# The Pool's residual maps wait, through a small VectorE read, for the last tile of the normed h

## The chip, the cores and the metric

One NeuronCore of a Trainium2 chip runs the whole program: TensorE (PE), VectorE (DVE), ScalarE (ACT), GpSimd (Pool) and the DMA queues, most of them issued by SyncE (SP). The metric is the device time of one execution in microseconds.

## The reference, cut to what matters

Two transformer blocks run one behind the other on 512 tokens and 256 context tokens, 1024 wide. The change touches only the first block, of two layers. Each layer has a token mixer, an MLP and two LayerNorms that sit on the residual sum:

```
for l in range(2):
    sh1, sc1, g1, sh2, sc2, g2 = split(silu(c) @ w_mod[l] + b_mod[l])
    h = x * (1 + sc1) + sh1                      # and the context alike
    y, yc = token_mixers(h, hc, ...)
    x = layer_norm(ALPHA * x + g1 * y, ln1_g[l], ln1_b[l])
    h = x * (1 + sc2) + sh2
    x = layer_norm(ALPHA * x + g2 * (relu(h @ w_fc1[l])**2 @ w_fc2[l]), ln2_g[l], ln2_b[l])
```

So each LayerNorm gives two things: the modulated h, which the next matmuls read at once, and the new x, which is needed only when the next residual sum is formed.

## The kernel before

Activations lie transposed: eight tiles of 128 channels, and tokens along the free axis. The residual stream R is eight such tiles (768 tokens in layer 0, 512 in layer 1), packed into four or three big tiles (`self.stream`). The tokens are normalised in groups of 256: three groups behind the attention of layer 0, two behind that of layer 1. Matmul operands are pairs hi and lo (`whi`/`wlo` for weights, `hn` for the normed h), and every product takes three matmuls. A weight piece goes through a `wraw` load on SP's queue, a cast to `whi` on ScalarE (L90) and a subtraction to `wlo` on VectorE (L91).

For each group, `LayerNorm` adds the tiles up on Pool (L161, into `ns`), TensorE forms the mean (`lm`, L167 and L168), VectorE and, for two tiles of the eight, Pool subtract it (L174), ScalarE squares (`lq`, L176), and TensorE sums (`lv`, L180). Then `normed` makes h out of each tile: VectorE L1071, ScalarE L1072 (hi), VectorE L1073 (lo). `residual` does not run at once; it puts a function into `self.later`, of two Pool operations that turn R in place into ALPHA times the new x:

```
nc.gpsimd.tensor_tensor(out=z, in0=z, in1=r, op=ALU.mult)             # L1080
nc.gpsimd.tensor_scalar(out=z, in0=z, scalar1=self.dcol(slot, m), ...)  # L1081
```

Below, such a pair of Pool operations is called a pair. `catch_up` runs what is in `self.later`. It is called in `fc1_piece` and at the end of a layer, and finds work there in three places of the program:

- **Place A**, in front of the MLP of layer 0: 24 pairs (three groups of eight).
- **Place B**, between layer 0 and the projections of layer 1: 16 pairs, each with a store of its R tile to the scratch tensor `xa` (128x256, SP's queue, L1422) behind it.
- **Place C**, in front of the MLP of layer 1: 16 pairs.

The engines' instructions are put in order by the scheduler of the tile framework when the kernel is built, out of program order, priorities (weights come first) and dependencies; on the chip each engine and each queue then goes through its list in order.

Names that matter behind the three places. In the MLP, `fc1_piece` makes an activation tile pair `act` out of h: ScalarE L934 (`r`) and L935 (`act`), VectorE L936 and L937. A modulation vector of a later step is computed beside the MLP, as a job of VectorE products: Pool copies one column (L564, from `act` into the buffer `wm`) before SP may load a piece of modulation weights into `wm` (L586), VectorE multiplies and sums it (L574), and L600 finishes the vector. `R<-f,modsb,R` (L973) adds fc2's result to R with the modulation `modsb`. `scale_alpha` (L1350, VectorE) writes the per-channel constants `der` that L1081 reads: slots 8 and 9 are written anew for layer 1 after place A's pairs of layer 0 have read them. Behind place B come the projections `pj`, whose rms norm sums (`pv`, L698) wait for squares of projected tiles.

Of the kernel before, what the change touches and what calls it, by code (L numbers as in the profile page):

```python
# [11 lines left out]
F32 = mybir.dt.float32  # L12
# [3 lines left out]
ALU = mybir.AluOpType  # L16
# [381 lines left out]
class Kernel:  # L398
# [540 lines left out]
    def fc1_piece(self, W, h, groups, pk, sides=(), n=1):  # L939

        ws = [W.get(ahead=n == 1 or i == 0) for i in range(n)]
        acts = [pk.pair() for _ in range(n)]
        pss = [self.P2("f1") for _ in range(n)]
        for i, (c0, c1) in enumerate(groups):
            for side in sides[i:i + 1]:
                self.drain(side)
                if i == len(sides) - 1:
                    self.catch_up()
            for k in range(8):
                for (wh, wl), ps in zip(ws, pss):  # L950
                    s = slice(k * 128, k * 128 + 128)
                    rs = [(c0, c1)] if c1 <= 512 or c0 >= 512 else [(c0, 512), (512, c1)]
                    self.mm3(ps, wh[:, s], wl[:, s], *h[k], rs, k == 0, k == 7)
                    for side in sides[i + 1:]:
                        self.adv(side)
        c0, c1 = groups[0][0], groups[-1][1]
        for act, ps in zip(acts, pss):
            self.relu2(act, ps, c0, c1)
            self.gate = act[0][:, c0:c0 + 1].bitcast(F32)
        return acts  # L960
# [122 lines left out]
                after()  # L1083
        self.later.append(f)

    def catch_up(self):
        while self.later:
            self.later.pop(0)()

# [276 lines left out]
    def block1(self):  # L1366
        nc, a = self.nc, self.a
        W = self.W = Stream(self, *a["stream"], 1)
        between = self.start1()
        h = next(between)  # L1370
        bg = self.bg

        def J(w, tiles, vecs, tag, bias):
            self.tags.add(tag)
            return self.mod_job(w, tiles, vecs, tag, bias)

        both0 = [(0, 0), (1, 1)]
        self.tags |= {"l0.g1", "l0.m2"}
        bg.append(self.mod_groups(range(4, 10), {5: "l0.g1", 9: "l0.m2"}))

        def vectors0():
            self.bcast(1, 1)
            yield

        bg.append(vectors0())
        bg.append(J(a["wmod0"], range(40, 48), both0, "l0.g2", "bmod0"))
        bg.append(J(a["wmod1"], range(0, 16), [(2, 0), (3, 1)], "l1.m1", "bmod1"))
        bg.append(J(a["wmod1"], range(16, 24), [(2, 0)], "l1.g1", "bmod1"))
        bg.append(J(a["wmod1"], range(24, 40), [(2, 0)], "l1.m2", "bmod1"))
        bg.append(J(a["wmod1"], range(40, 48), [(2, 0)], "l1.g2", "bmod1"))  # L1390

        def vectors():
            for slot, v in ((0, 2), (1, 3)):
                self.bcast(v, slot)
                yield

        bg.append(vectors())
        bg.append(J(a["wada0"], range(0, 16), [(4, 0), (5, 1)], "b0.m1", "bada0"))
        for l in range(2):
            last = l == 1  # L1400
            hn, z, gs, groups, sides, norm = self.layer1(l, h, W, between if l == 0 else None)
            h = None
            h2, hpk = [None] * 8, Packer(self, T, name="h")
            state = {}

            def finish(rng, ln, l=l, last=last, h2=h2, hpk=hpk, z=z):
                if last:
                    return self.to_block2(rng, ln, z, h2, hpk)
                if rng[0] == 0:
                    self.need("l1.m1")  # L1410
                    self.fold(4, 2, 0, 1, f"ln2g{l}", f"ln2b{l}")
                    self.fold(6, 3, 0, 1, f"ln2g{l}", f"ln2b{l}")
                    self.scale_alpha(10, f"ln2g{l}")
                    self.scale_alpha(11, f"ln2b{l}")
                s = 6 if rng[0] >= 512 else 4

                def f(m, t, r):
                    if h2[m] is None:
                        h2[m] = hpk.pair()
                    self.normed(h2, m, rng, t, r, s)  # L1420
                    if s == 4:
                        self.residual(m, t, r, 10, lambda: nc.sync.dma_start(out=a["xa"][:, m, rng[0]:rng[1]], in_=t))  # L1422
                return ln.finish(f)

            if last:
                hpk = Packer(self, 512, name="a")
                self.queue2()
            self.run(self.mlp(W, hn, z, gs, groups, sides, norm, finish, f"l{l}.g2"), *RATES[l])
            if last:
                self.need("ctxk")  # L1430
            for i, _ in enumerate(self.side):
                if last and i >= VSKIP and (i - VSKIP) % VEACH == 0:
                    for _ in range(VSTEP):
                        next(self.values, None)
            if last:
                for _ in self.values:
                    pass
            self.catch_up()
            h = h2
        return h  # L1440

# [845 lines left out]
```

## Time and profile before

| | us |
|---|---|
| three runs | 3006.62, 3000.3, 2999.19 |
| median | 3000.3 |
| the profiled execution | 3004.72 |
| its span in the profile | 3002.9 |
| busy in the span: PE, DVE, ACT, POOL | 2825.6 (94%), 1976.0 (66%), 1240.6 (41%), 668.1 (22%) |

The span is what the profiler saw from the first to the last instruction; the rest of the execution's 3004.72 us lies around it. Times in the rows further down are microseconds from the start of the span. Place A lies at 491 to 542, place B at 1075 to 1114 and place C at 1455 to 1491.

### The profile page before, as it was taken

How to read it: one execution, taken by the hardware profiler on the slowest of the kernel's cores; microseconds unless marked ns; L12 is line 12 of the kernel's file. 1: busy time of each engine (PE TensorE's matmuls, PEld its weight loads, DVE VectorE, ACT ScalarE, POOL GpSimd, SP SyncE). 2: the span in 40 equal slices, each digit the busy share in tenths (PEclk: the TensorE clock that was granted, in tenths of full speed). 3: DMA queues.
4: the chain of work that ended last, by engine and by line, in shares of the span. 5: the costliest groups of instructions: out<-in, count | busy, mean ns of one | idle time of the engine just before them, and what ended most of it. 6: DMA issues, size and time to landing. Idle time of an engine off the chain costs nothing.

```text
span 3002.9 us, 40272 instructions
## 1 busy us (share of the span) xinstructions
PE 2825.6 (94%) x15140; PEld 2377.2 (79%) x15140; DVE 1976.0 (66%) x3177; ACT 1240.6 (41%) x2250; POOL 668.1 (22%) x800
## 2 busy tenths in 40 slices
PE   8988999999999989889999999988899999999998
PEld 5877778888888867778887788766788888888887
DVE  3677766676555676886686566677976754664445
ACT  3477663312222244776332333433653223443223
POOL 1134346201000151343511122343310100200001
PEclk9999999999999999999999999999999999899999
DMA  6022221344443321012255555233115542222322
GB/s 251 32 67 70 75 92 41 111 151 165 140 134 126 113 71 39 17 36 79 72 176 173 181 195 179 99 123 109 65 64 195 198 138 99 75 71 98 98 98 71
DMA packets 103072, 329.52 MB, mean 110 GB/s; under 512 B 11708, under 2 KB 18812, under 8 KB 102877
## 3 DMA queue, kind: packets, MB, share of 16 engines
q1 hardware_dynamic: 102300, 325.24, 32.3%
q8 instruction: 120, 1.97, 0.3%
q10 hardware_dynamic: 576, 1.71, 0.2%
q14 instruction: 76, 0.61, 0.1%
HBM read 307.76 MB, written 13.37 MB: 107 GB/s over the span
## 4 chain that ended last, share of the span: by engine, by line
PE 74%; DVE 10%; ACT 5%; issue 5%; DMA 3%; POOL 3%; SPq 0%; DVEq 0%; POOLq 0%; ACTq 0%
PE f L645 47%; PE pj L645 6%; PE op L645 6%; PE s L257 3%; PE acc L346 2%; PE pt L303 1%; DVE st L270 1%; ACT p L280 1%; DVE ptl L335 1%; DVE h L1071 1%; DVE wlo L91 1%; ACT pth L330 1%; PE ms L1095 1%; PE pp L1983 1%; PE lv L180 1%
## 5 line engine op out<-in xcount | busy, mean ns | idle before, releaser
L90 ACT CAST whi<-wraw 128x1024 fp32r<-128x1024 f32 x342 | 358.1, 1047 | 1206.6 <-PE f L645 1004.0
L645 PE MATMUL f<-hn,whi 128*128 128x512 f32 (+1 forms) x2688 | 715.3, 364 | 7.0 <-ACT hn L1072 5.8
L91 DVE TENSOR_TENSOR wlo<-wraw,whi 128x1024 fp32r<-128x1024 f32 x342 | 426.4, 1247 | 341.7 <-ACT whi L90 335.0
L645 PE MATMUL f<-act,whi 128*128 128x512 f32 x2240 | 609.3, 369 | 8.1 <-DVE R L973 8.1
L645 PEld LDWEIGHTS f<-hn,whi 128*128 128x128 f32 x2688 | 467.5, 191 | 90.5 <-ACT hn L1072 7.0
L645 PEld LDWEIGHTS f<-act,whi 128*128 128x128 f32 x2240 | 388.7, 188 | 82.9 <-DVE R L973 9.3
L645 PE MATMUL f<-hn,wlo 128*128 128x512 f32 (+1 forms) x1344 | 446.6, 362 | 0.0
L645 PE MATMUL f<-act,wlo 128*128 128x512 f32 x1120 | 375.8, 368 | 0.0
L973 DVE SCALAR_TENSOR_TENSOR R<-f,modsb,R 128x512 f32<-128x512 f32 (+1 forms) x280 | 188.7, 692 | 132.5 <-PE f L645 132.5
L645 PEld LDWEIGHTS f<-hn,wlo 128*128 128x128 f32 x1344 | 238.7, 191 | 39.1
L564 POOL COPY wm<-act 128x1 f32<-128x1 f32 x152 | 83.4, 555 | 824.2 <-ACT act L935 415.6
L574 DVE SCALAR_TENSOR_TENSOR wm<-wm,sbc 128x1024 f32<-128x1024 f32 x152 | 186.7, 1229 | 121.1 <-DMA wm<-wada_in 79.0
L645 PE MATMUL pj<-h,whi 128*128 128x512 f32 (+1 forms) x864 | 243.4, 382 | 9.3 <-ACT h L651 5.4
L645 PEld LDWEIGHTS f<-act,wlo 128*128 128x128 f32 x1120 | 194.3, 188 | 36.2
L645 PEld LDWEIGHTS pj<-h,whi 128*128 128x128 f32 x864 | 151.2, 193 | 48.0 <-issue 6.9
L289 POOL TENSOR_SCALAR p<-p,st 128x768 f32<-128x768 f32 (+2 forms) x160 | 130.8, 821 | 228.7 <-DVE st L287 179.4
L270 DVE TENSOR_REDUCE st<-s 128x1 f32<-128x768 f32 (+3 forms) x176 | 156.1, 889 | 34.7 <-PE s L257 24.6
L211 POOL TENSOR_TENSOR ns<-ns,rq 128x256 f32<-128x256 f32 x54 | 46.1, 865 | 590.7 <-ACT rq L203 590.0
L335 DVE TENSOR_TENSOR ptl<-pt,pth 128x256 fp32r<-128x256 f32 (+3 forms) x304 | 153.2, 534 | 18.0 <-ACT pth L330 14.4
L303 PE MATMUL pt<-ident,p 128*128 128x128 f32 x816 | 126.2, 284 | 26.2 <-DVE ptl L335 10.5
L280 ACT ACTIVATE p<-s,st 128x768 f32<-128x768 f32 (+2 forms) x160 | 125.9, 789 | 45.1 <-DVE st L270 35.3
L330 ACT CAST pth<-pt 128x256 fp32r<-128x256 f32 (+3 forms) x304 | 129.7, 472 | 30.2 <-PE pt L303 27.5
(368 smaller groups left out, 4689.0 us busy)
## 6 DMA issues: line engine op xcount, KB each, us to landing
wraw<-fc_in SPq DMA_DIRECT2D x128, 512.0 KB, 3.3
wraw<-mlp_in SPq DMA_DIRECT2D x128, 512.0 KB, 3.3
wm<-wada_in SPq DMA_DIRECT2D x96, 512.0 KB, 3.7
wm<-wmod_in SPq DMA_DIRECT2D x56, 512.0 KB, 4.1
wraw<-win_in SPq DMA_DIRECT2D x24, 512.0 KB, 3.2
wm<-wmodk_in SPq DMA_DIRECT2D x24, 512.0 KB, 4.2
wn<-wmodk_in SPq DMA_DIRECT2D x16, 512.0 KB, 8.9
wraw<-wout_in SPq DMA_DIRECT2D x16, 512.0 KB, 3.3
```

The lines of the kernel that those rows point to most:

```text
L90: nc.scalar.copy(out=hi[:, 0:n], in_=t[:, 0:n])
L91: nc.vector.tensor_tensor(out=lo[:, 0:n], in0=t[:, 0:n], in1=hi[:, 0:n].bitcast(F32), op=ALU.subtract)
L257: nc.tensor.matmul(self.s[:, a:b], lhsT=q, rhs=kk[:, k0:k0 + b - a], start=i == 0, stop=end)
L270: nc.vector.tensor_reduce(out=self.st[:, 0:self.nq], in_=s, axis=AX.X, op=ALU.max, negate=True)
L280: nc.scalar.activation(out=self.p[:, b * m:b * m + m], in_=self.s[:, self.c0 + b * m:self.c0 + b * m + m], func=AF.Exp, bias=st[:, b:b + 1 ...
L289: nc.gpsimd.tensor_scalar(out=self.p[:, b * m:b * m + m], in0=self.p[:, b * m:b * m + m], scalar1=st[:, 6 + b:7 + b], scalar2=1.0, op0=ALU ...
L303: nc.tensor.transpose(self.pt[t // w][:, t % w * 128:t % w * 128 + 128], self.p[:, t * 128:t * 128 + 128], k.ident)
L330: self.k.nc.scalar.copy(out=pr.hi[:, s0:s0 + c, q0:q0 + nq], in_=src)
L335: self.k.nc.vector.tensor_tensor(out=pr.lo[:, s0:s0 + c, q0:q0 + nq], in0=src, in1=pr.hi[:, s0:s0 + c, q0:q0 + nq].bitcast(F32), op=ALU.su ...
L574: nc.vector.scalar_tensor_tensor(out=junk, in0=t, scalar=1.0, in1=s, op0=ALU.mult, op1=ALU.mult, accum_out=dst)
L645: self.nc.tensor.matmul(ps[:, c0:c1], lhsT=w, rhs=x[:, c0:c1], start=first and n == 0, stop=last and n == 2)
L973: nc.vector.scalar_tensor_tensor(out=zz, in0=ps[:, c0:c1], scalar=g(m0 + mi), in1=zz, op0=ALU.mult, op1=ALU.add)
```

## The change

`catch_up` takes the normed h. If there is something in `self.later`, VectorE first reads a strided sample of each big tile of R (one column for each 256 tokens) together with as many columns of the last lo tile of h, and writes their sum to a small tile `gate` that nobody reads. The Pool's writes to R then have to wait for these reads, and the reads for the last L1073.

```
-    def catch_up(self):
+    def catch_up(self, h):
+
+        if self.later:
+            lo, left = h[7][1], 8
+            for t in self.stream:
+                c, n = min(left, t.shape[1]), t.shape[2]
+                w = c * n // 256
+                left -= c
+                x = t[:, 0:c, 0:n:256]
+                o, l = (y.rearrange("p (a b) -> p a b", a=c) for y in (self.S2("gate")[:, 0:w], lo[:, n - 256:n - 256 + w]))
+                self.nc.vector.tensor_tensor(out=o, in0=x, in1=l.bitcast(F32), op=ALU.add)
         while self.later:
             self.later.pop(0)()
```

The two calls become `self.catch_up(h)` in `fc1_piece` and `self.catch_up(h2)` at the layer's end. There are eleven gates: four at A, four at B, three at C (128x6, the last of C 128x4). Behind the new lines all line numbers grow by ten (L1350 becomes L1360, L1422 becomes L1432).

Pool at the start of place A, before; L161 and L174 belong to the LayerNorm of the groups that follow, L1080 and L1081 are the pairs:

```order
L1080 TENSOR_TENSOR R<-R,ns 128x256
L1081 TENSOR_SCALAR R<-R,der 128x256
L1080 TENSOR_TENSOR R<-R,ns 128x256
L1081 TENSOR_SCALAR R<-R,der 128x256
L1080 TENSOR_TENSOR R<-R,ns 128x256
L1081 TENSOR_SCALAR R<-R,der 128x256
L1080 TENSOR_TENSOR R<-R,ns 128x256
L1081 TENSOR_SCALAR R<-R,der 128x256
L161 TENSOR_TENSOR ns<-ns,R 128x256
L174 TENSOR_TENSOR R<-R,ns 128x256 x2
L1080 TENSOR_TENSOR R<-R,ns 128x256
L1081 TENSOR_SCALAR R<-R,der 128x256
```

And after, where the last LayerNorm operations stand in front of the first pair:

```order
L161 TENSOR_TENSOR ns<-ns,R 128x256 x3
L174 TENSOR_TENSOR R<-R,ns 128x256 x2
L161 TENSOR_TENSOR ns<-ns,R 128x256 x2
L174 TENSOR_TENSOR R<-R,ns 128x256 x2
L1080 TENSOR_TENSOR R<-R,ns 128x256 x2
L1081 TENSOR_SCALAR R<-R,der 128x256 x2
L1080 TENSOR_TENSOR R<-R,ns 128x256 x2
L1081 TENSOR_SCALAR R<-R,der 128x256 x2
L1080 TENSOR_TENSOR R<-R,ns 128x256 x2
L1081 TENSOR_SCALAR R<-R,der 128x256 x2
```

All 24 pairs have moved behind the LayerNorm operations of all three groups, and two pairs each have been folded into one another; the L564 copies follow the 24th as before. Places B and C have moved in the same way.

VectorE at the end of place A, before; the last L1073 and what follows it:

```order
L1073 SCALAR_TENSOR_TENSOR hn<-h_5389,der,hn 128x256
L1073 SCALAR_TENSOR_TENSOR hn<-h_5396,der,hn 128x256
L1350 TENSOR_SCALAR der<-colsb 128x8 x2
L91 TENSOR_TENSOR wlo<-wraw,whi 128x1024
L936 TENSOR_TENSOR r<-r 128x768 x2
L937 TENSOR_TENSOR act<-r,act 128x768 x2
L91 TENSOR_TENSOR wlo<-wraw,whi 128x1024 x2
L936 TENSOR_TENSOR r<-r 128x768
```

And after:

```order
L1073 SCALAR_TENSOR_TENSOR hn<-h_5389,der,hn 128x256
L1073 SCALAR_TENSOR_TENSOR hn<-h_5396,der,hn 128x256
L1096 TENSOR_TENSOR gate<-R,hn 128x6 x4
L91 TENSOR_TENSOR wlo<-wraw,whi 128x1024
L936 TENSOR_TENSOR r<-r 128x768 x2
L937 TENSOR_TENSOR act<-r,act 128x768 x2
L91 TENSOR_TENSOR wlo<-wraw,whi 128x1024
L1360 TENSOR_SCALAR der<-colsb 128x8 x2
L91 TENSOR_TENSOR wlo<-wraw,whi 128x1024
L936 TENSOR_TENSOR r<-r 128x768
```

The four gates are new, and the two L1350 writes of `der` (now L1360), which have to wait for the last pair, have moved from in front of six operations to behind them. TensorE and ScalarE keep their order.

SP's queue at place B, before; `xa` is the store of R, `wraw` a load of weights:

```order
L72 DMA wraw<-win_in 128x1024 x4
L1422 DMA xa<-R 128x256 x3
L72 DMA wraw<-win_in 128x1024
L1422 DMA xa<-R 128x256 x7
L72 DMA wraw<-win_in 128x1024
L1422 DMA xa<-R 128x256 x6
L72 DMA wraw<-win_in 128x1024 x6
L72 DMA wraw<-wq_in 128x1024
```

And after:

```order
L72 DMA wraw<-fc_in 128x1024
L72 DMA wraw<-win_in 128x1024 x7
L1432 DMA xa<-R 128x256 x16
L72 DMA wraw<-win_in 128x1024 x5
L72 DMA wraw<-wq_in 128x1024
L72 DMA wraw<-wkv_in 128x512
```

The sixteen stores, which lay between the weight loads in three lots, are now one lot: one more weight load stands ahead of them, and the next five and all behind these stand behind the last store.

## Rows read from the trace of the kernel before

**Rows 1.** The page: the chain that ended last; the weight loads (KB, us to landing).
```profile
PE 74%; DVE 10%; ACT 5%; issue 5%; DMA 3%; POOL 3%; SPq 0%; DVEq 0%; POOLq 0%; ACTq 0%
...
wraw<-fc_in SPq DMA_DIRECT2D x128, 512.0 KB, 3.3
```

**Rows 2.** Stretches: length, busy PE, PEld, DVE, ACT, POOL, granted clock, DMA share, GB/s.
```profile
491.00:538.00 47.00, 40.57 (x274) 37.04 (x273) 45.73 (x74) 24.05 (x52) 44.89 (x49) 0.96 0.13 46
1075.00:1114.00 39.00, 30.42 (x119) 20.99 (x120) 38.63 (x66) 21.78 (x48) 30.69 (x35) 0.91 0.25 81
1114.00:1128.00 14.00, 14.00 (x75) 11.33 (x74) 6.40 (x8) 7.19 (x11) 0.00 (x0) 1.00 0.33 114
1455.00:1486.00 31.00, 25.22 (x156) 22.80 (x156) 28.63 (x47) 15.02 (x32) 28.64 (x32) 0.89 0.16 52
```

**Rows 3.** VectorE's groups between 491.3 and 537.9: xcount | busy us, mean ns | idle before.
```profile
L1071 DVE SCALAR_TENSOR_TENSOR h<-R,der,ns 128x256 f32<-128x256 f32 x22 | 15.8, 754 | 0.1
L1073 DVE SCALAR_TENSOR_TENSOR hn<-h,der,hn 128x256 fp32r<-128x256 f32 x24 | 14.9, 647 | 0.3 <-ACT hn L1072 0.3
L174 DVE TENSOR_TENSOR R<-R,ns 128x256 f32<-128x256 f32 x12 | 6.7, 596 | 0.0
```

**Rows 4.** Timeline, VectorE and then Pool: start, us, engine, line, out<-in, count, idle before.
```profile
506.76 1.33 DVE L91 TENSOR_TENSOR wlo<-wraw,whi 128x1024 fp32r<-128x1024 f32 x1 [0.32 <-ACT whi L90]
...
1107.78 0.96 DVE L1073 SCALAR_TENSOR_TENSOR h<-h,der,h 128x256 fp32r<-128x256 f32 x1
...
1109.60 0.47 DVE L1071 SCALAR_TENSOR_TENSOR h<-R,der,ns 128x256 f32<-128x256 f32 x1
1110.00 0.47 DVE L1073 SCALAR_TENSOR_TENSOR h<-h,der,h 128x256 fp32r<-128x256 f32 x1
...
506.97 1.73 POOL L1080 TENSOR_TENSOR R<-R,ns 128x256 f32<-128x256 f32 x1
...
1107.55 0.90 POOL L1080 TENSOR_TENSOR R<-R,ns 128x256 f32<-128x256 f32 x1
1108.56 0.85 POOL L1081 TENSOR_SCALAR R<-R,der 128x256 f32<-128x256 f32 x1
```

**Rows 5.** Timeline of Pool, the last residual pairs of place A.
```profile
539.45 0.74 POOL L1080 TENSOR_TENSOR R<-R,ns 128x256 f32<-128x256 f32 x1
...
540.82 0.75 POOL L1080 TENSOR_TENSOR R<-R,ns 128x256 f32<-128x256 f32 x1
```

**Rows 6.** Timeline behind place A: VectorE, ScalarE, Pool, VectorE, TensorE.
```profile
536.46 1.35 DVE L1073 SCALAR_TENSOR_TENSOR hn<-h,der,hn 128x256 fp32r<-128x256 f32 x2 [0.17 <-ACT hn L1072]
542.27 0.25 DVE L1350 TENSOR_SCALAR der<-colsb 128x8 f32<-128x8 f32 x2 [4.45 <-POOL R L1081]
...
543.56 1.82 DVE L936 TENSOR_TENSOR r<-r 128x768 f32<-128x768 f32 x2
...
567.29 0.85 ACT L935 ACTIVATE act<-r 128x768 fp32r<-128x768 f32 x1
...
568.20 1.09 POOL L564 COPY wm<-act 128x1 f32<-128x1 f32 x2 [25.96 <-ACT act L935]
...
607.51 0.15 DVE L600 TENSOR_TENSOR modsb<-modsb,colsb 128x8 f32<-128x8 f32 x1
...
608.77 1.65 PE L645 MATMUL f<-act,whi 128*128 128x512 f32 x4 [5.53 <-DVE R L973]
```

**Rows 7.** Timeline at place B: VectorE's last lo, ScalarE's cast, TensorE's pv.
```profile
1112.96 0.88 DVE L1073 SCALAR_TENSOR_TENSOR h<-h,der,h 128x256 fp32r<-128x256 f32 x2
...
1128.77 1.05 ACT L90 CAST whi<-wraw 128x1024 fp32r<-128x1024 f32 x1
...
1139.45 1.12 PE L698 MATMUL pv<-sq,ones 128*128 128x512 f32 x2 [0.75 <-ACT sq L705]
```

**Rows 8.** Timeline at place C: VectorE's last lo, Pool's next copies.
```profile
1482.79 1.72 DVE L1073 SCALAR_TENSOR_TENSOR hn<-h,der,hn 128x256 fp32r<-128x256 f32 x2
...
1504.61 0.80 POOL L564 COPY wm<-act 128x1 f32<-128x1 f32 x2 [13.72 <-ACT act L935]
```

More of the change, by code (lines that the diff above doesn't have):

```diff
@@ L947, in fc1_piece @@
                 if i == len(sides) - 1:
-                    self.catch_up()
+                    self.catch_up(h)
             for k in range(8):
@@ L1437, in block1 @@
                     pass
-            self.catch_up()
+            self.catch_up(h2)
             h = h2
```

## The prediction, as it went on record

> **What bounds the kernel now.** I read the page first, then the stretches around the three places, then the timelines of the engines there. TensorE stands on 74% of the chain, VectorE on 10%, Pool on 3% [rows 1]: a microsecond counts where TensorE stands still or runs at a lower clock. Around the places it does. In the 47 us of place A it is busy for 40.57, in the 39 us of B for 30.42, in the 31 us of C for 25.22, while VectorE is busy nearly throughout; behind B it is busy for 14.00 of 14.00 us [rows 2]. [...] So VectorE, which makes h, is the limit in these stretches, and what TensorE could win at most is its idle time and its clock: A 6.4 + 0.04 x 47 = 8.3 us, B 8.6 + 0.09 x 39 = 12.1, C 5.8 + 0.11 x 31 = 9.2.
>
> Why is VectorE slow there? At the end of B a 128x256 L1073 beside a running pair takes 0.96 us; the pair ends at 1109.41, and the L1071 that starts at 1109.60 takes 0.47, with the next one 0.40 us behind it [rows 4]. Pool and VectorE slow each other down, and the change takes the pairs out of VectorE's way.
>
> **What the change brings, until the last lo.** In A, L1071, L1073 and L174 are busy for 15.8 + 14.9 + 6.7 = 37.4 us in 58 operations [rows 3]; at 0.40 they need 23.2, so at most 14.2 us can go. Pool is busy for 44.89 us in A, 30.69 in B, 28.64 in C [rows 2]; at the same rate B can lose 9.7 and C 9.1. Not all of that comes: sums of TensorE, squares of ScalarE and the L161 and L174 that stay on Pool still stand between. I take 10 us in A, 8.8 in B, 8 in C. The last lo ends at 537.81 in A [rows 6], 1113.84 in B [rows 7] and 1484.51 in C [rows 8]; it would end at 527.8, 1105.0 and 1476.5. TensorE then stands some 8, 8 and 7 us ahead. Eleven gates cost little: the nearest row is a small two-input operation at 0.15 us [rows 6], four of them 0.4 with overlap, at most 0.6; below nothing they can't be, and no work is in their way.
>
> **What the pairs cost afterwards.** Only now does Pool begin, and what stood beside its pairs no longer hides them. A pair alone takes 540.82 - 539.45 = 1.37 us [rows 5]; beside VectorE 1109.41 - 1107.55 = 1.86 [rows 4]. So 24 pairs take 32.9 to 44.6 us, 16 take 21.9 to 29.8. The 0.49 us more come with about two VectorE operations of 0.40, that is 0.6 us for each us of VectorE's own work; a 1024-wide `wlo` of 1.33 us held an L1080 up to 1.73 against 0.74 [rows 4, 5], 0.75 for each us. I take 0.6, and keep 0 and 1 as ends.
>
> **Place A.** Behind the gates VectorE does two `wlo` and four 128x768 operations, then waits at L1350 for the last pair. One of the four is 0.91 us [rows 6], a `wlo` 1.2: 6.1 us. Pool ends at 527.8 + 0.4 + 32.9 + 0.6 x 6.1 = 564.8 instead of 542.3. L1350 waited 4.45 us before [rows 6]; now it waits some 25. Behind it in VectorE's queue stands the `wlo` of the fifth fc1 piece, and its `wraw` buffer is what SP needs for the next load, and that piece's cast is what ScalarE has ahead of the fifth piece's `act`. From the last pair it is 0.25 (L1350) + 1.2 (`wlo`) + 3.3 (load [rows 1]) + 1.05 (cast [rows 7]) + 2 x 0.85 (relu and square [rows 6]) = 7.5 us to that `act`, the one for which Pool's L564 copies wait. Before, they start at 568.20 right behind the `act` of 567.29 [rows 6]; now at 572.3. All of the modulation job hangs on them: 39.4 us later L600 ends, and TensorE, which had waited 5.53 us for it, goes on at 608.77 [rows 6]. So TensorE's 8 us in hand are lost there, and 4.1 us more. **A: +4.1.** The point where nothing is lost is a last pair at 560.7. With 0 and the full 14.2 us Pool ends at 523.6 + 0.4 + 32.9 = 556.9: -3.8. With 44.6 us for the pairs it ends at 572.8: +12.
>
> **Place B.** Here sixteen stores move with the pairs, and SP's queue stands behind the last of them: weight loads that before went between wait for it. Who waits for them: the cast of a fourth projection piece, on ScalarE at 1128.77, and, since ScalarE's and VectorE's queues are in order, all behind it up to TensorE's `pv` at 1139.45, 10.7 us later, which already waits 0.75 us [rows 7]. VectorE's work beside the pairs is 6.40 us in 14 [rows 2]. Pool ends at 1105.0 + 0.4 + 21.9 + 0.6 x 6.4 = 1131.1; a load and its issue take 3.7 us; the cast comes at 1134.8 instead of 1128.77. TensorE's 8 us are lost again, and 6 more. **B: +6.0.** The even point is a last pair at 1125.1. Ends: 1104.1 + 0.4 + 21.9 = 1126.4, +1.3; with 29.8 for the pairs 1135.2, +10.
>
> **Place C.** There is no L1350 and no store. Pool ends between 1476.5 + 0.3 + 21.9 = 1498.7 and, with 29.8, 1506.6; I take 1503. The next Pool work are the L564 copies at 1504.61, which waited for `act` for 13.72 us [rows 8]. TensorE keeps its 7 us unless these copies are late next; they would be 1.6 us earlier, not 7, and fc2's additions stand between that job's products on VectorE. I take half-way between 1.6 and 7. **C: -4** (-8 to 0).
>
> **The sum.** 4.1 + 6.0 - 4 = +6.1 us on the profiled execution's 3004.7 us (its span and 1.8 around it). It lies 4.4 us above the median of the runs, so I add the difference to the median: 3000.3 + 6.1 = 3006.4, called 3006. A change under 0.3% (9 us) can't be told from none here: forecast no change that can be measured, leaning to slower.
>
> [...] An L1080 that met a `wlo` of VectorE took 1.73 us instead of 0.74 [rows 4, 5], so Pool was held about three quarters of the `wlo`. [...]
>
> **The rivals.**
> 1. *Nothing lost behind the pairs (faster).* Pool runs its pairs alone at 1.37 us and VectorE wins all that it can: -3.8 in A, +1.3 in B, -8 in C: -10.5, 2990 us. For it speaks that VectorE will mostly stand still at L1350; against it the 6 us of long operations right behind the gates. It decides when Pool ends before 560.7 and 1125.1.
> 2. *Pool is held up for the full length of VectorE's work (slower).* With 1 in place of 0.6, Pool ends at 567.2 in A (+6.5) and at 1133.7 in B (+8.6), and in C behind 1504.61, -1: +14, 3014 us. For it speaks the `wlo` row.
> 3. *The change doesn't do what it says.* VectorE is slow for another reason, and the last lo comes no earlier: Pool ends at 537.8 + 33.3 = 571.1 (+10) and 1113.8 + 22.3 = 1136.1 (+11), C about 0: +21, 3021 us. The step from 0.96 to 0.47 us as Pool stops [rows 4] speaks against it.
>
> **How the numbers follow.** Mine 0.60, rival 1 0.18, rival 2 0.18, rival 3 0.04. Mine alone reaches from -2 to +13, 2998 to 3013; a fifth of it, 0.12, lies over +9. Slower 0.12 + 0.18 + 0.04 = 0.34; faster 0.15, most of rival 1; same 0.51. The range holds rival 1 at its edge and rival 2 with its upper ends: 2990 to 3018.
>
> **What the profile after would show.** Right: L1071 and L1073 at 0.47 us in all three places, last lo 8 to 10 us earlier; pairs back to back behind the gates; L1350 waiting over 20 us for Pool; the copies of 568.20 no earlier in spite of TensorE's head start, TensorE waiting over 10 us at L973 or for `wlo` in A; SP standing behind the stores and `pv` late in B. Wrong would be a Pool that ends before 560.7 or 1125.1 (then it is faster), `wraw` buffers that let the loads run ahead of the stores, or lo tiles that come no earlier.

## The result, and the profile after

The changed kernel takes 3019.59 us (median of seven runs, 3014.17 to 3029.69), the kernel before 3002.61 (seven runs, 2999.19 to 3007.69). The ratio is 1.006, with an interval of 1.0044 to 1.0076: 13 to 23 us slower. The forecast was 3006, no change that can be measured, in a range from 2990 to 3018; the measured time lies above it. The profiled execution of the changed kernel is the slowest of the seven, 3029.69 us.

On the page the chain that ended last has four points less of TensorE (74% before) and two more of Pool (3% before) [rows 1]:

```profile
PE 70%; DVE 11%; POOL 5%; issue 5%; ACT 5%; DMA 4%; SPq 0%; DVEq 0%; POOLq 0%; ACTq 0%
```

The front of the change came as described. Here are the stretches up to the last lo (length, busy PE, PEld, DVE, ACT, POOL, clock, DMA share, GB/s), which answer to [rows 2]:

```profile
495.00:534.00 39.00, 37.10 (x268) 34.48 (x267) 36.44 (x78) 23.45 (x52) 9.96 (x10) 1.00 0.17 55
1089.00:1122.00 33.00, 29.07 (x128) 22.17 (x127) 31.00 (x72) 23.22 (x51) 3.94 (x5) 0.95 0.13 44
1475.00:1500.00 25.00, 22.08 (x160) 20.65 (x160) 22.69 (x52) 14.49 (x33) 2.71 (x4) 1.00 0.19 64
```

Pool is busy for 10, 4 and 3 us there instead of 45, 31 and 29, TensorE idles for 1.9, 3.9 and 2.9 us where it idled for 6.4, 8.6 and 5.8, and its clock is 1.00, 0.95 and 1.00. What follows is where the time went. Place A in the timeline of the changed kernel, which answers to [rows 6]; the constants `der` are now written in L1360, the gate is L1096:

```profile
531.24 0.89 DVE L1073 SCALAR_TENSOR_TENSOR hn<-h,der,hn 128x256 fp32r<-128x256 f32 x2 [0.18 <-ACT hn L1072]
532.16 1.00 DVE L1096 TENSOR_TENSOR gate<-R,hn 128x6 f32<-128x6 f32 x4
...
567.28 0.25 DVE L1360 TENSOR_SCALAR der<-colsb 128x8 f32<-128x8 f32 x2 [22.54 <-POOL R L1081]
...
532.41 1.44 POOL L1080 TENSOR_TENSOR R<-R,ns 128x256 f32<-128x256 f32 x2 [15.27 <-DVE gate L1096]
...
574.66 1.09 POOL L564 COPY wm<-act 128x1 f32<-128x1 f32 x2 [7.41 <-ACT act L935]
...
571.96 1.06 ACT L90 CAST whi<-wraw 128x1024 fp32r<-128x1024 f32 x1 [16.05 <-DMA wraw<-fc_in]
...
573.75 0.85 ACT L935 ACTIVATE act<-r 128x768 fp32r<-128x768 f32 x1
...
614.18 1.65 PE L645 MATMUL f<-act,whi 128*128 128x512 f32 x4 [13.94 <-DVE R L973]
```

The pairs run from 532.41 to 567.25, just ahead of L1360. VectorE waits 22.54 us for the last of them, the fifth piece's weights land late (ScalarE waits 16.05 us for `wraw`), `act` is there at 574.60, and only then come the copies. TensorE's wait at the modulation job has grown from 5.53 to 13.94 us.

Place B, which answers to [rows 7]:

```profile
1119.58 0.87 DVE L1073 SCALAR_TENSOR_TENSOR h<-h,der,h 128x256 fp32r<-128x256 f32 x2
...
1144.08 1.09 POOL L1081 TENSOR_SCALAR R<-R,der 128x256 f32<-128x256 f32 x2
...
1123.71 21.80 SPq L1432 DMA_DIRECT2D xa<-R  x16
1145.61 13.71 SPq L72 DMA_DIRECT2D wraw<-win_in  x4
...
1149.36 1.04 ACT L90 CAST whi<-wraw 128x1024 fp32r<-128x1024 f32 x1 [12.85 <-DMA wraw<-win_in]
...
1160.03 2.08 PE L698 MATMUL pv<-sq,ones 128*128 128x512 f32 x2 [14.68 <-ACT sq L705]
```

SP stands behind the sixteen stores from 1123.71 to 1145.5. The next load starts behind them, ScalarE's cast waits 12.85 us for it, and TensorE 14.68 us at `pv`. The two `pv` matmuls take 2.08 us where they took 1.12: the clock has fallen in the wait. It is granted at 1.00 from 1145 to 1148, at 0.50 from 1152 to 1163 and at 0.81 from 1163 to 1170 (0.50 at first, 1.00 from 1166); in the kernel before it is 1.00 from 1139.4 on, behind a wait of 0.75.

Place C, which answers to [rows 8]; the VectorE rows in the middle belong to the sine chain of the second block's filter (L1575) and to the MLP's `act` (L937):

```profile
1498.73 0.89 DVE L1073 SCALAR_TENSOR_TENSOR hn<-h,der,hn 128x256 fp32r<-128x256 f32 x2 [0.18 <-ACT hn L1072]
...
1526.48 0.68 DVE L937 TENSOR_TENSOR act<-r,act 128x512 fp32r<-128x512 f32 x1
1527.08 0.68 DVE L1575 SCALAR_TENSOR_TENSOR fhd<-fhd,sn 64x512 f32<-64x512 f32 x1
...
1499.90 1.43 POOL L1080 TENSOR_TENSOR R<-R,ns 128x256 f32<-128x256 f32 x2 [14.71 <-DVE gate L1096]
...
1524.80 7.38 POOL L1081 TENSOR_SCALAR R<-R,der 128x256 f32<-128x256 f32 x1
...
1537.60 0.30 POOL L564 COPY wm<-act 128x1 f32<-128x1 f32 x2
...
1537.81 0.80 SPq L586 DMA_DIRECT2D wm<-wada_in  x2
1538.71 0.38 SPq L72 DMA_DIRECT2D wraw<-fc_in  x1
...
1544.32 1.04 ACT L90 CAST whi<-wraw 128x1024 fp32r<-128x1024 f32 x1 [11.66 <-DMA wraw<-fc_in]
...
1545.91 1.22 PE L645 MATMUL f<-act,whi 128*128 128x512 f32 x2 [6.28 <-ACT r L934]
```

Pool's sixteen pairs take from 1499.90 to 1537.60, 37.7 us, where the forecast had 21.9 to 29.8. One L1081 takes 7.38 us, while VectorE issues its 512-wide operations every 0.60 us. The copies come at once behind the last pair, SP's modulation loads at 1537.81 behind the copies, and a weight load behind those; ScalarE waits 11.66 us for it and TensorE 6.28. Here too the clock falls in the wait: 1.00 from 1541 to 1543, 0.50 from 1546 to 1550 and 0.83 from 1550 to 1554, where TensorE had no wait and a clock of 1.00 in the kernel before.

**Place by place.** TensorE's order is the same in all kernels, so its n-th matmul can be set against the n-th of the kernel before. The difference of their starts, at a place's end less at its beginning, is what the place costs; its lowest value on the way is what had been gained before the pairs began. Beginnings and ends are 470 and 620 (A), 1060 and 1150 (B), 1448 and 1570 (C) on the clock of the trace before; "MLP" is layer 0's, from 630 to 1050, where no kernel differs. All in us, one profiled execution each; where a kernel has no gate at a place the table has -0.5 to +0.1, so half a us means nothing in it:

```
                A (lowest)     B (lowest)     C (lowest)     MLP
changed       +2.5 (-7.3)    +8.4 (-7.9)    +4.9 (-6.1)    +7.6
gate_a        +2.6 (-7.3)     0.0            0.0           +7.6
gate_b        -0.5           +8.0 (-8.1)     0.0           +7.6
gate_c         0.0            0.0           +3.9 (-6.1)    +7.6
no_pairs      -7.6           -7.9           -6.1            0.0
gate_a_slots  -1.6 (-7.3)     0.0            0.0            0.0
gate_b_poolq  -0.5           -0.4 (-8.1)     0.0           +7.6
gate_c_half   -0.4            0.0           -1.8            0.0
all_fixes     -0.9 (-7.3)    -0.2 (-7.9)     0.0           +7.6
gate_a_pace   -3.2 (-7.4)     0.0            0.0            0.0
best          -3.2 (-7.4)     0.0           -1.8            0.0
gates_blind   +0.1            0.0            0.0            0.0
```

The three places of the changed kernel add up to 2.5 + 8.4 + 4.9 = +15.8 us, within the measured 13 to 23. The MLP column is no effect of the change: gate_b and gate_c run the same instructions there as the kernel before. It is a second pace of TensorE (last section) and makes up 7.6 of the 25.0 us by which the span of the changed kernel's profiled execution, 3027.9 us, is longer than that before. The small rest comes from stretches where no kernel differs: TensorE is 4.3 us late before A begins, for one.

### The profile page after: what moved, and what is told of

Read it like the earlier page. It is cut to its first block, busy times and chain, and to the rows that moved or that the text cites. A ratio compares the mean times of both kernels' runs of the same rounds, so it can differ in the third digit from the quotient of the medians.

```text
span 3027.9 us, 40262 instructions
## 1 busy us (share of the span) xinstructions
PE 2834.8 (94%) x15140; PEld 2385.3 (79%) x15140; DVE 1958.3 (65%) x3188; ACT 1238.2 (41%) x2250; POOL 667.0 (22%) x800
## 4 chain that ended last, share of the span: by engine, by line
PE 70%; DVE 11%; POOL 5%; issue 5%; ACT 5%; DMA 4%; SPq 0%; DVEq 0%; POOLq 0%; ACTq 0%
PE f L645 43%; PE pj L645 6%; PE op L645 6%; PE s L257 3%; PE acc L346 2%; POOL R L1081 2%; PE pt L303 1%; POOL R L1080 1%; DVE st L270 1%; DVE ptl L335 1%; DVE wlo L91 1%; ACT p L280 1%; DMA wm<-wada_in 1%; PE lv L180 1%; PE ms L1105 1%
## 5 line engine op out<-in xcount | busy, mean ns | idle before, releaser
L645 PE MATMUL f<-act,whi 128*128 128x512 f32 x2240 | 615.8, 373 | 22.9 <-DVE R L973 16.6
L564 POOL COPY wm<-act 128x1 f32<-128x1 f32 x152 | 86.5, 576 | 788.6 <-DVE wm L574 386.1
L330 ACT CAST pth<-pt 128x256 fp32r<-128x256 f32 (+3 forms) x304 | 129.5, 472 | 33.1 <-PE pt L303 29.3
```

The source lines that it names most:

```text
L330: self.k.nc.scalar.copy(out=pr.hi[:, s0:s0 + c, q0:q0 + nq], in_=src)
L645: self.nc.tensor.matmul(ps[:, c0:c1], lhsT=w, rhs=x[:, c0:c1], start=first and n == 0, stop=last and n == 2)
```

## The experiments

The time of each kernel is given as its ratio to the kernel before, run on the same chip, with a 95% interval; 0.1% is 3 us. The runs of one kernel spread over some 10 to 20 us, so the ratios can't tell 3 us from none, and the place table carries the small differences.

**One place at a time.** Three kernels keep the gate at one place; a fourth keeps all gates and has no pairs.

```
+        place = "B" if end else "A" if self.stream and self.stream[0].shape[2] == 768 else "C"
-        if self.later:
+        if self.later and place in "A":          # "B", "C"
```

gate_a. 

> The gate at place A alone. By the mended account (front gain of about 8 us, lost again at the modulation job that Pool starts late): TensorE waits about 13 us in front of fc2's first sums, against 5.5 before, and the time is +2 us (0 to +4). By the rival that a long wait of TensorE leaves the matmuls of the following MLP at the slower of two paces (six 512-column matmuls' starts 1.06 us apart in place of 1.04): +9 us, with most of it between that wait and place B.

Measured 1.0003 (0.9987 to 1.0019); place A +2.6. TensorE waited 13.85 us there, as expected.

gate_b. 

> The gate at place B alone. Mended account: the sixteen stores hold SP's queue until the last pair, the cast that feeds pv is some 7 us late, TensorE waits about 14 us at pv: +9 us (6 to 11). If the stores were no hindrance, the front gain stays: -7 us.

Measured 1.0027 (1.0010 to 1.0044); place B +8.0, with a wait of 14.47 us at `pv`.

gate_c. 

> The gate at place C alone. Mended account: Pool's 16 pairs take 35 us and more beside VectorE's sine chain of the filter, the copies come some 12 us late, SP stands at the modulation loads and the weight loads behind them: +4 us (+2 to +7). As first predicted (16 pairs at 1.37 to 1.86 us, end before 30 us): -4 us.

Measured 1.0007 (0.9989 to 1.0024); place C +3.9, with a wait of 5.99 us.

no_pairs leaves the two Pool operations of `residual` out:

```
         def f():
-            nc.gpsimd.tensor_tensor(out=z, in0=z, in1=r, op=ALU.mult)
-            nc.gpsimd.tensor_scalar(out=z, in0=z, ...)
             if after is not None:
```

> All three gates, and the residual's two Pool operations left out, so that R keeps the centred sum: the residual is not normalised. Every front gain stays and nothing comes after it: -7 in A, -8 in B, -6 in C, and the wait for the modulation job in A shrinks as well: -21 us (-16 to -28). If VectorE is slow at the three places for another reason than the pairs: 0.

Measured 0.9932 (0.9909 to 0.9955), 14 to 27 us faster; -7.6, -7.9 and -6.1 at the places. So Pool's pairs are what slows VectorE in front of the last lo, and the gains in front are real at all three places. Each single gate loses its gain and more at its own place and nowhere else. The rival pace, set by the long wait at A, falls: gate_b and gate_c, whose wait at A is that of before, show the slower pace in the MLP too. Nor can the slower pace belong to these kernels in every execution and the faster to the kernel before: gate_c would then come to +3.9 + 7.6 = 11.5 us, 1.0038, and its interval ends at 1.0024.

**What the reads themselves cost.** The gates read the lo tile alone, so that Pool waits for nothing.

```
-                self.nc.vector.tensor_tensor(out=o, in0=x, in1=l.bitcast(F32), op=ALU.add)
+                self.nc.vector.tensor_tensor(out=o, in0=l.bitcast(F32), in1=l.bitcast(F32), op=ALU.add)
```

> All eleven VectorE reads, but of the lo tile alone, so that Pool waits for nothing: the price of the reads by themselves. 11 x 0.25 us on an engine that is the limit in front of each place: +0 to +2.5 us, with the places at +0.5 each; the rest of the changed kernel's +17 us is then the waiting.

Measured 0.9999 (0.9981 to 1.0018), and at most 0.1 us at any place: the eleven reads are free or nearly so; the forecast had 0.3 to 0.6 us at a place.

**What makes the work behind A late.** Layer 1's constants get slots of their own, so that VectorE has no write to wait with.

```
-            self.scale_alpha(8, f"ln1g{l}")
-            self.scale_alpha(9, f"ln1b{l}")
+            self.scale_alpha(8 + 10 * l, f"ln1g{l}")
+            self.scale_alpha(9 + 10 * l, f"ln1b{l}")
...
-                self.residual(m, t, r, 8)
+                self.residual(m, t, r, 8 + 10 * l)
```

> The gate at A alone, and layer 1's two constants of the residual in slots 18 and 19 of der, so that VectorE has no write left that waits for the last pair. If that wait (22.5 us in the changed kernel) is what makes act and the copies late: Pool ends as before at about 563, act is ready earlier, the copies start at the last pair's end instead of 7.4 us behind it, and the modulation job ends some 5 us earlier than before: -5 us against before (-3 to -8). If Pool itself is what is late: +2 as with the gate alone.

Measured 0.9995 (0.9980 to 1.0010); place A -1.6, 4.2 us better than the gate alone, not the 7 that were expected. Pool and TensorE in its timeline:

```profile
569.65 0.30 POOL L564 COPY wm<-act 128x1 f32<-128x1 f32 x2
...
605.70 1.65 PE L645 MATMUL f<-act,whi 128*128 128x512 f32 x4 [10.15 <-DVE R L973]
```

The copies now start with the last pair's end and no longer 7.4 us behind it. But the last pair itself came 7 us later than in the changed kernel, since VectorE, free to go on, stood in Pool's way: beside its operations two L1081 take up to 4.34 us, where two without it take 1.09. Set against each other on the clock of the trace before, the copies start at 570.0 here and at 570.4 in the changed kernel: the wait of VectorE and the slower Pool make them equally late. Most of the 4.2 us came behind the copies: VectorE's first product, which waits for the modulation load, starts 3.5 us behind the copies' start (569.65 to 573.14) instead of 6.8 (574.66 to 581.48). In the changed kernel SP is at weight loads until 575.00 and issues the modulation loads at 575.66, 1.0 us behind the copies' start. Whether this makes the difference was not tried. TensorE still waits 10.15 us. So the next kernel let ScalarE make the first two copies:

```
-        for j in tiles[:2]:
-            load(j)
+        for j in tiles[:2]:
+            load(j, tag in ("l0.g2",))
...
+            if act:
+                self.nc.scalar.copy(out=t[:, 0:1], in_=self.gate)
```

> The gate at A with slots of their own, and the first two copies of the l0.g2 modulation job made by ScalarE, right behind the act that they read, in place of Pool behind its last pair. If the late job is all that A loses: the copies start at about 560 instead of 569.7, TensorE's wait in front of fc2's first sums falls from 10 to about 4 us, and place A comes to -7 us (-5 to -8). If Pool still holds the job, by its later copies or by slowing the products on VectorE: -2 as with the slots alone.

Measured 0.9991 (0.9973 to 1.0008); place A -3.2, neither the -7 nor the -2. ScalarE, Pool and TensorE:

```profile
558.79 0.28 ACT L565 COPY wm<-act 128x1 f32<-128x1 f32 x2
...
565.75 6.73 POOL L1084 TENSOR_SCALAR R<-R,der 128x256 f32<-128x256 f32 x2
...
574.91 0.30 POOL L567 COPY wm<-act 128x1 f32<-128x1 f32 x2
...
603.57 1.65 PE L648 MATMUL f<-act,whi 128*128 128x512 f32 x4 [9.71 <-DVE R L976]
```

The first two copies come at 558.79, some 9 us earlier when the two executions are set against each other. The third is Pool's, and it stands behind the last pair until 574.91, because the job's own products on VectorE now hold Pool up: two L1084 (L1081 of the other kernels) take 6.73 us. TensorE's wait falls by 0.4 us only. The job as a whole, not its first copy, is tied to Pool's last pair.

**What makes the work behind B late.** Pool issues the stores on its own queue:

```
-   self.residual(m, t, r, 10, lambda: nc.sync.dma_start(out=a["xa"][...], in_=t))
+   self.residual(m, t, r, 10, lambda: nc.gpsimd.dma_start(out=a["xa"][...], in_=t))
```

> The gate at B alone, with the sixteen stores issued by Pool on its own queue, so that SP's weight loads have nothing ahead of them. If the stores were what held them: the front gain of 8 us stays and nothing is late, -8 us (-5 to -12). If Pool's pairs themselves are the loss, by what they do to VectorE: +3 or more.

Measured 0.9995 (0.9980 to 1.0009); place B -0.4 instead of +8.0. The stores on SP's queue were the 8.4 us between, but the gain of 8.1 in front is lost all the same. VectorE, Pool and TensorE behind the gate:

```profile
1138.47 2.31 DVE L780 TENSOR_TENSOR u<-u,w 32x512 f32<-32x512 f32 x1
...
1131.68 1.13 POOL L1432 DMA_DIRECT2D xa<-R  x2
...
1143.02 2.08 PE L698 MATMUL pv<-sq,ones 128*128 128x512 f32 x2 [5.22 <-ACT sq L705]
```

VectorE's operations of `pv`'s chain run beside the pairs now: a 32x512 L780 takes 2.31 us, where it took 0.68 before. `pv` still waits 5.22 us and starts 3.7 us ahead of the kernel before; behind it the two `pv` matmuls take 2.08 us, as in the changed kernel at its clock of 0.50, where they took 1.12 before, and the first `wlo` matmul starts 2.73 us behind the first `pv` instead of 1.43. That is 1.3 of the 3.3 us that are lost again there; the rest was not taken apart. So both rivals named in the expectation hold in part: the queue was one part of the loss, Pool's work beside VectorE is the other. How much of that other part is the pairs' own was not separated, for the remedy has a price too: two stores take Pool 1.13 us to issue, and its work behind the gate lasts 40.4 us (1113.20 to 1153.64) instead of 24.4 in the changed kernel.

**What makes the work behind C late.** The gate samples the second group's columns alone, so that eight pairs run as before and eight wait.

```
-                w = c * n // 256
+                w = c * (n - 256) // 256
-                x = t[:, 0:c, 0:n:256]
+                x = t[:, 0:c, 256:n:256]
```

> The gate at C alone, and only for the second group of 256 tokens: eight pairs run beside VectorE as before, eight wait. If it is the length of Pool's work behind the gate that makes the copies late: Pool ends some 15 to 20 us earlier than with sixteen, before the sine chain, about half of the front gain stays, and nothing is lost: -3 us (-1 to -5). If any wait of Pool at C costs: +4 as with the gate at C.

Measured 0.9994 (0.9975 to 1.0012); place C -1.8 instead of +3.9. Pool's last pair and the copies:

```profile
1488.30 1.96 POOL L1081 TENSOR_SCALAR R<-R,der 128x256 f32<-128x256 f32 x2
1493.86 0.80 POOL L564 COPY wm<-act 128x1 f32<-128x1 f32 x2 [3.61 <-ACT act L935]
```

Pool is done 3.6 us before the copies are due, ahead of the sine chain, and nothing behind it is late. So it is the length of Pool's work beside VectorE that decides at C, not the waiting as such.

**Together.** all_fixes has the gates at A and B with both remedies:

> The gates at A and B with both remedies (slots of their own in A, stores on Pool's queue in B), none at C. The sum of the two single runs' expectations: -13 us (-8 to -18). If the gains at A and B don't add up, because layer 0's MLP lies between them and other waits of TensorE take what A gives: -8.

Measured 0.9991 (0.9975 to 1.0008); -0.9 and -0.2 at the places, so the two remedies only give back what the gates cost. best has gate_a_pace and gate_c_half in one:

> As gate_a_pace, and at C the gate for the second group alone. The sum over the places: -7 in A, 0 in B, -2 in C: -9 us (-4 to -12) against before.

Measured 0.9989 (0.9972 to 1.0006); -3.2 and -1.8 at the places. They add up, but the time can't be told from that of the kernel before; it is clear of the changed kernel's 1.0044 and more.

**The disputed price by itself.** A kernel of its own, with four forms of VectorE work:

```
for i in range(40): v.scalar_tensor_tensor(out=d[:, s], in0=w[:, s], scalar=k[:, 0:1], in1=b[:, s], ...)   # 128x256
for i in range(30): v.scalar_tensor_tensor(out=d[q], in0=d[q], scalar=0.01, in1=b[q], ...)                 # 64x512, a chain
for i in range(16): v.tensor_tensor(out=d[:, s], in0=w[:, s], in1=b[:, s], op=ALU.subtract)                # 128x1024
for i in range(40): v.tensor_scalar(out=d[:, s], in0=ps[:, 0:256], scalar1=w[:, 0:1], ...)                 # from PSUM
```

> A kernel of another kind, that leaves out all of the reference's work: eight residual pairs on Pool, alone and beside VectorE that works back to back in four forms. If VectorE's reads of two SBUF inputs hold Pool for their full length (the second rival): beside 40 operations of 128x256 from SBUF the sum of both engines' own times, 8 x 1.37 + 40 x 0.40 = 27 us until both are done; beside the 64x512 chain and the 128x1024 operations Pool ends only some 11 us behind the last of them or is held up by most of their 18 us; beside operations with one input, from PSUM, both run as alone, 11 us and 16 us. If the price is 0.6 for each us: Pool's pairs end after 11 + 0.6 x 11 = 18 us.

Timeline of VectorE: 40 of 128x256 alone and beside the pairs, 30 of the 64x512 chain alone and beside, 16 of 128x1024 alone and beside, 40 from PSUM beside; then Pool: the pairs alone, beside the 128x256, beside the chain, beside the 128x1024, beside those from PSUM:

```profile
26.71 15.91 DVE L26 SCALAR_TENSOR_TENSOR d<-w,k,b 128x256 f32<-128x256 f32 x40
...
49.51 20.79 DVE L26 SCALAR_TENSOR_TENSOR d<-w,k,b 128x256 f32<-128x256 f32 x40
...
77.70 21.47 DVE L32 SCALAR_TENSOR_TENSOR d<-d,b 64x512 f32<-64x512 f32 x30
...
106.50 26.73 DVE L32 SCALAR_TENSOR_TENSOR d<-d,b 64x512 f32<-64x512 f32 x30
...
140.19 18.25 DVE L37 TENSOR_TENSOR d<-w,b 128x1024 f32<-128x1024 f32 x16
...
165.34 20.95 DVE L37 TENSOR_TENSOR d<-w,b 128x1024 f32<-128x1024 f32 x16
...
198.32 15.75 DVE L42 TENSOR_SCALAR d<-ps,w 128x256 f32<-128x256 f32 x40
...
12.34 1.40 POOL L47 TENSOR_TENSOR za<-za,r 128x256 f32<-128x256 f32 x2 [11.90 <-DVE za L54]
...
21.05 1.09 POOL L48 TENSOR_SCALAR za<-za,k 128x256 f32<-128x256 f32 x2
...
49.68 1.75 POOL L47 TENSOR_TENSOR zc<-zc,r 128x256 f32<-128x256 f32 x2 [27.54 <-DVE zc L54]
...
62.20 1.89 POOL L48 TENSOR_SCALAR zc<-zc,k 128x256 f32<-128x256 f32 x2
...
106.22 1.96 POOL L47 TENSOR_TENSOR ze<-ze,r 128x256 f32<-128x256 f32 x2 [42.13 <-DVE ze L54]
...
120.72 1.95 POOL L48 TENSOR_SCALAR ze<-ze,k 128x256 f32<-128x256 f32 x2
...
165.50 3.29 POOL L47 TENSOR_TENSOR zg<-zg,r 128x256 f32<-128x256 f32 x2 [42.84 <-DVE zg L54]
...
186.52 1.40 POOL L47 TENSOR_TENSOR zg<-zg,r 128x256 f32<-128x256 f32 x2
...
198.49 1.41 POOL L47 TENSOR_TENSOR zh<-zh,r 128x256 f32<-128x256 f32 x2 [7.06 <-DVE zh L54]
...
207.20 1.09 POOL L48 TENSOR_SCALAR zh<-zh,k 128x256 f32<-128x256 f32 x2
```

Eight pairs alone take 9.8 us (12.34 to 22.14), 1.22 each. Beside operations from PSUM they take the same 9.8 us (198.49 to 208.29), and VectorE's 40 take 15.75, as long as 40 of such shape from SBUF alone (15.91); the PSUM form was not run alone.

Beside 128x256 from SBUF both suffer: Pool 14.4 us (49.68 to 64.09), VectorE 20.79. In these 14.4 us VectorE did about 24 of its 40 (the other 16 took the 6.2 us after it at 0.40), 9.6 us of work, so each us of VectorE cost Pool 4.6 / 9.6 = 0.5. Beside the 64x512 chain Pool takes 16.4 us (106.22 to 122.67), and VectorE did about 15 of its 30 in them, 10.9 us of work: 6.6 / 10.9 = 0.6. Beside 128x1024 the first four pairs take 21 us (165.50 to 186.52) instead of 4.9, and VectorE only 2.7 us more than alone: 16.1 of its 18.25 us, 0.9 for each.

So neither expectation holds for all forms: in this one execution the price rises from 0.5 over 0.6 to 0.9 as VectorE's operations grow from 256 over 512 to 1024 columns (the 512-wide ones on 64 partitions, each waiting for the one before). The full price would have had both engines done with the 128x256 after 27 us; they were after 20.8.

## Why the prediction was wrong

The sign leaned the right way, and A and B lost where it was expected; but C, forecast as a gain, lost too, and the sum of +6.1 us was 10 too low. To set the steps of the prediction against the changed kernel's profile, its times are shifted back by the lag that TensorE has already when the place begins: 4.3 us at A, 14.6 at B, 21.4 at C.

- *The front.* Forecast: last lo at 527.8, 1105.0 and 1476.5, TensorE 8, 8 and 7 us ahead. Measured: 527.8, 1105.9 and 1478.2; 7.3, 7.9 and 6.1 ahead. Right, and no_pairs shows the cause. The third rival falls with it.
- *Place A.* Forecast: last pair 564.8, copies 572.3, +4.1. Measured: 563.0, 570.4, +2.5. Nearly right in sum, by two errors that partly cancel: the pairs, folded into one another, take 9.8 / 8 = 1.22 us alone (ports), not 1.37, so 24 of them 29.3 of the measured 34.8 us; the other 5.5 are 0.9, not 0.6, for each of VectorE's 6.1 us. The copies come 7.4 us behind the last pair, as forecast (7.5). What the prediction did not see is that Pool is as late without VectorE's wait: gate_a_slots takes the wait away, and the copies come at 570.0, hardly earlier; gate_a_pace shows that Pool's later copies hold the job too.
- *Place B.* Forecast: last pair 1131.1, cast 1134.8, +6.0. Measured: 1130.6, 1134.8, `pv` at 1145.5 (+6.0) and +8.4 at the place's end. The step was right to half a microsecond, by the same two errors (16 pairs took 24.4 us, the forecast 25.7); the term was 2.4 short, since the clock, which fell from 1.00 to 0.50 in the wait of 14.68 us, was left out: the `pv` matmuls took 2.08 us for 1.12, at a granted clock of 0.50. gate_b_poolq shows the stores' part.
- *Place C.* This is the step that failed: "Pool ends between 1498.7 and 1506.6; I take 1503", from a pair of at most 1.86 us, "TensorE keeps its 7 us unless these copies are late next". Measured: the last pair at 1516.2, 2.36 us a pair, the copies 12 us later than before instead of 1.6 earlier, +4.9 instead of -4. At A and B the prediction counted VectorE's work beside the pairs, 6.1 and 6.4 us; at C it did not count it, and took as a ceiling a pair beside 128x256 operations. VectorE has some 24 us of work beside the pairs there: six 1024-wide operations of 1.2, 21 two-input ones 512 wide of 0.68, and five of 0.4 to 0.8 with one. At the prediction's own price that alone would have put Pool's end at 1476.5 + 0.3 + 21.9 + 0.6 x 24 = 1513.1, behind the 1504.61 of the copies. As measured, the 24 us cost Pool 37.7 - 16 x 1.22 = 18.2 us, about 0.8 for each, between the 0.6 and 0.9 that ports shows for 512 and 1024 columns. gate_c brings the loss back alone (+3.9), and in gate_c_half, where half of the pairs run earlier and the other half end ahead of the sine chain, nothing is lost. The fallen clock behind TensorE's wait (0.50, then 0.83), which the sum has nowhere, is in the +4.9 as well.
- *The price of 0.6.* It was read from one pair beside about two operations of VectorE. The trace has about three beside it (they start at 1107.78, 1108.66 and 1109.06, with the end of one in front), 1.2 us of work, which makes 0.4. That 0.6 lies between the 0.5 and 0.9 of ports is luck.
- *The rivals.* The second one, that Pool is held up for the full length of VectorE's work, gave 3014 and comes nearest of those whose mechanism is seen in the runs (the third's 3021 is nearer to the measured time, by luck: its lo tiles come no earlier, and here they came 6 to 10 us earlier). Its price is nearly right for the long operations at A (0.9) and C (0.8), but it counts VectorE's work at C no more than the main line does, and had Pool's copies at C only a little late. In ports Pool lost nothing beside VectorE's operations from PSUM (eight pairs 9.8 us, as alone), and beside the 128x1024 operations it was held for 0.9 of their length; beside 128x256 operations both engines took about one and a half times as long (Pool 14.4 us for 9.8, VectorE 0.6 us an operation for 0.40), and neither was held for the whole length of the other's work.

The first rival (nothing lost behind the pairs) falls at all three places.

## What to carry to other kernels

Work that is taken out of the way of the critical engine has to go somewhere: before it is moved behind a point, list what stands behind its last instruction on its own engine, on the queue that its stores use, and on every engine that has a write waiting for its reads, and compare their slack with the length of the moved work (here SP's weight loads stood behind the stores until 1145.5, and VectorE 22.54 us at L1360). Price that length beside the work that will be next to it, not beside the work that it left: here a folded pair costs 1.22 us alone, 1.80 beside 128x256 operations (ports), 2.36 beside the row at C and 5.25 beside a row of 128x1024 operations (ports). Where the whole lot is too long, moving a part of it may keep a part of the gain: gate_c_half kept 1.8 of 6.1 us at C, in one execution, too little for the times of the runs to show.

## What the runs showed of the hardware

TensorE ran the same row of matmuls at two paces. In the kernel before, and in gate_b, whose instructions here are the same, one step of six matmuls apart (three of 512 columns and three of 256, not six of 512 as the expectation of gate_a has it):

```profile
761.00 0.85 PE L645 MATMUL f<-act,whi 128*128 128x512 f32 x4
...
762.04 0.86 PE L645 MATMUL f<-act,whi 128*128 128x512 f32 x4
```

```profile
760.94 0.87 PE L645 MATMUL f<-act,whi 128*128 128x512 f32 x4
...
762.00 0.88 PE L645 MATMUL f<-act,whi 128*128 128x512 f32 x4
```

From the first `whi` of one step to the first of the next it is 1.04 us in the one and 1.06 in the other, all through layer 0's MLP: 7.6 us over 420. The changed kernel has the slower pace too (1.06 from 764.01 to 765.07), and its granted clock there is no lower: 1.00 from 650 to 1060, as in the kernel before from 640 to 1040. Of the eleven experiments that run this network, five had the slower pace there in their profiled execution, as the changed kernel had, and six the faster one, and nothing lay between: the same 400 us of the MLP (400.2 at the faster pace) take 407.5 at the slower one. VectorE and ScalarE run alike in both (a 1024-wide cast takes 1.05 us). What sets the pace was not tried. With it a single execution may be 8 us off, as much as the effects that were looked for, which is why the places were measured one by one.

VectorE held Pool through a dense row: at C one L1081 took 7.38 us (two take 1.09 beside an idle VectorE) while VectorE's 512-wide rows follow each other every 0.60 us at 0.68 each, no longer than in the kernel before, where Pool is idle beside them. Issue without a gap was not enough for it: the 128x256 operations of ports came every 0.40 us too when alone, and beside them two Pool operations of L1081's form took 1.89 us, not 1.09.

A store that Pool issues costs Pool itself some 0.57 us (two L1432 take 1.13 in gate_b_poolq), which delays the pairs behind it: the next two pairs start at 1132.83, right behind the two stores issued from 1131.68 on.
